# im2col, 3x3: one instruction for the copies of two channels, and one first load in place of two

## The chip, the cores and the metric

The kernel runs on one core of a Trainium2 chip. The metric is the device time of one execution in microseconds (us). The core has a vector engine (VectorE, DVE in the profile), a scalar engine (ScalarE, ACT), GpSimd (POOL), a sync engine (SyncE, SP) that here only issues transfers, and a matrix engine that this kernel doesn't use. Sixteen DMA engines move data between device memory (HBM) and the on-chip memory of 128 partitions. A transfer that SyncE or ScalarE issues is spread over all sixteen, eight partitions to each, and it is recorded in packets. Each of the sixteen has its own completion write, and whoever waits for a transfer waits for all sixteen.

## The reference

The input `x` has 16 images of 64 channels, 32 by 32, in float32. The output has, for every image and channel, nine planes of 30 by 30: plane `ki*3 + kj` is the channel's image shifted by `ki` rows and `kj` columns. Nothing is computed; every input element is copied up to nine times.

```
h_out = h - kernel_size + 1          # 30
w_out = w - kernel_size + 1          # 30
for b in range(batch):
    col_idx = 0
    for i in range(h_out):
        for j in range(w_out):
            patch = x[b, :, i:i + kernel_size, j:j + kernel_size].copy()
            cols[b, :, col_idx] = patch.ravel()
            col_idx += 1
```

The input is 4.19 MB and the output 33.18 MB.

## The kernel before

The 16 x 64 = 1024 channels are laid over the 128 partitions, eight consecutive channels to a partition (`CPP` = 8). A partition's input is one run of 32,768 bytes in HBM, and its output one run of 259,200 bytes. The whole input fits into one tile, `in_tile` (partition, channel, row, column). The output is built in four rounds, each for a pair of channels, in `out_tile` (partition, 2 channels, 9 planes, 30, 30): 64,800 bytes in a partition. There are two such buffers (line 26), so round 2 can't write until the store of round 0 is through, and round 3 waits for that of round 1.

The loads (lines 33 to 41). There are three: channel 0 of each partition, issued by SyncE; channel 1, issued by ScalarE; and channels 2 to 7, issued by SyncE. The first two are called `first` and are moved by hand, after the program is compiled, to the front of the program on their engines, ahead of the barrier with which all engines start (lines 88 to 103). The third is issued after that barrier.

The copies (lines 49 to 70). In a round, for each of the two channels `s`, ScalarE copies the three planes with `ki` = 1 in one instruction (line 55, 2700 elements in a partition). VectorE copies two planes of `ki` = 0 and two planes of `ki` = 2 (line 57, 1800 elements each). Planes 2 and 8, the third ones of `ki` = 0 and 2, are left. For the first channel VectorE takes both in one instruction (line 61); for the second, VectorE takes plane 2 (line 65) and ScalarE plane 8 (line 68). That makes six instructions on VectorE (9,900 elements) and three on ScalarE (6,300 elements), or nine in all for the 18 planes. The helper `planes` (lines 43 to 47) builds the source: `n` windows of 30 by 30 that lie `step` elements apart in one channel's image. The order is the one written, with no scheduler (line 28).

A wait is put on the first instruction that needs it: in round 0, the first channel's copies wait for the first load alone, and those of the second channel for the second load too. The copies of round 1 wait for the third load.

The store (line 71) is issued by SyncE once both engines have finished a round, one transfer of 8.29 MB. SyncE's queue thus holds, in this order: the load of channel 0, the load of channels 2 to 7, and four stores. ScalarE's holds the load of channel 1 only.

Of the kernel before, what the change touches and what calls it, by code (L numbers as in the profile page):

```python
# [1 line left out]

# [3 lines left out]


def _im2col(ctx, tc, x, K, out):


    nc = tc.nc
    P = nc.NUM_PARTITIONS

    B, C, H, W = x.shape
    HO = H - K + 1
    WO = W - K + 1
    KK = K * K
    assert out.shape == (B, C * KK, HO * WO)
    CPP = B * C // P
    assert CPP * P == B * C and C % CPP == 0 and CPP % 2 == 0 and K == 3  # L20

    x_v = x.rearrange("b (cp c2) h w -> (b cp) (c2 h w)", c2=CPP)
    out_v = out.rearrange("b (cp c2 kk) n -> (b cp) c2 (kk n)", c2=CPP, kk=KK)

    in_pool = ctx.enter_context(tc.tile_pool(name="in_pool", bufs=1))
    out_pool = ctx.enter_context(tc.tile_pool(name="out_pool", bufs=2))

    ctx.enter_context(tc.manual_schedule())

    in_tile = in_pool.tile([P, CPP, H, W], x.dtype, name="in_tile")  # L30
    in_flat = in_tile.rearrange("p c h w -> p (c h w)")

    def load(queue, r0, r1):

        return queue.dma_start(
            out=in_flat[:, r0 * W : r1 * W],
            in_=x_v[:, r0 * W : r1 * W],
        )

    first = load(nc.sync, 0, H), load(nc.scalar, H, 2 * H)  # L40
    load(nc.sync, 2 * H, CPP * H)

    def planes(c, ki, kj, n, step):

        w = in_tile[:, c, ki : ki + HO, kj : kj + WO]
        part, row, col = [list(d) for d in w.ap]
        return bass.AP(w.tensor, w.offset, [part, [step, n], row, col])

    for c in range(0, CPP, 2):
        out_tile = out_pool.tile([P, 2, KK, HO, WO], x.dtype, name="out_tile")  # L50


        for s in range(2):
            o = out_tile[:, s]
            nc.scalar.copy(out=o[:, K : 2 * K], in_=planes(c + s, 1, 0, K, 1))  # L55
            for ki in (0, 2):
                nc.vector.tensor_copy(  # L57
                    out=o[:, ki * K : ki * K + 2], in_=planes(c + s, ki, 0, 2, 1)
                )
            if s == 0:  # L60
                nc.vector.tensor_copy(  # L61
                    out=o[:, 2:KK:6], in_=planes(c + s, 0, 2, 2, 2 * W)
                )
            else:
                nc.vector.tensor_copy(  # L65
                    out=o[:, 2], in_=in_tile[:, c + s, 0:HO, 2 : 2 + WO]
                )
                nc.scalar.copy(  # L68
                    out=o[:, 8], in_=in_tile[:, c + s, 2 : 2 + HO, 2 : 2 + WO]
                )  # L70
        nc.sync.dma_start(  # L71
            out=out_v[:, c : c + 2].rearrange("p c n -> p (c n)"),
            in_=out_tile.rearrange("p c kk i j -> p (c kk i j)"),
        )
    return first


def kernel(
    tc: tile.TileContext,
    x: bass.AP,  # L80
    kernel_size: bass.AP,
    out: bass.AP,
):
    with ExitStack() as ctx:
        first = _im2col(ctx, tc, x, int(kernel_size), out)


    tc.close()
    tc.compile()  # L89
    blocks = tc.nc.main_func.blocks  # L90
    for load in (f.ins for f in first):
        home = next(
            b for b in blocks if any(i.name == load.name for i in b.instructions)
        )
        home.instructions = [i for i in home.instructions if i.name != load.name]
        head = list(blocks[0].instructions)
        at = next(
            k
            for k, i in enumerate(head)
            if i.engine == load.engine and type(i).__name__ == "InstDrain"  # L100
        )
        head.insert(at, load)
        blocks[0].instructions = head


# [1 line left out]
_INS = ['x', 'kernel_size']  # L107
_OUTS = [((16, 576, 900), 'float32')]

_NUMBERS = {'kernel_size': 3}  # L110


# [26 lines left out]
```

## Time and profile before

| | us |
|---|---|
| four runs | 91.31, 91.50, 91.51, 91.51 (median 91.50) |
| the profiled execution | 91.51 |
| its span, first to last instruction | 89.7 |
| VectorE busy / ScalarE busy | 22.6 (25%) / 23.8 (27%) |
| moved by the DMA engines | 37.37 MB, a mean of 417 GB/s over the span |

The span leaves out what lies around the first and the last instruction, 1.8 us here. In the rows of groups a line has the source line, the engine, the operation, the tiles, the shape (partitions x elements) and the count; behind the first bar the busy time of all in us and the mean duration of one in ns, behind the second the idle time just before them and what ended it. In the timeline a row has its start and its length in us, then the engine, the line and the operation; rows of one kind are merged, and a bracket says how long the engine had been idle and what ended that.

The DMA issues of the page, with the median time from issue to landing:

```profile
## 6 DMA issues: line engine op xcount, KB each, us to landing
out_dram<-out_tile SPq DMA_DIRECT2D x4, 8100.0 KB, 32.4
in_tile<-in_x_dram SPq DMA_DIRECT2D x1, 3072.0 KB, 11.4
in_tile<-in_x_dram SPq DMA_DIRECT2D x1, 512.0 KB, 4.4
in_tile<-in_x_dram ACTq DMA_DIRECT2D x1, 512.0 KB, 4.8
```

A store's time to landing holds the time that it waits in the queue behind the transfer before it.

### The profile page before, as it was taken

The numbers are of one execution on the slowest core, as the hardware profiler recorded it, in microseconds if no ns is written. First come the engines' busy times: TensorE is split into PE (matmuls) and PEld (weight loads), VectorE is DVE, ScalarE is ACT, GpSimd is POOL, SyncE is SP. The second block draws the span as 40 slices with busy tenths as digits, with TensorE's granted clock in tenths as the row PEclk, the third lists the DMA queues.
The fourth block names the chain that finished last, engine by engine and source line by source line (L and its number), as shares of the span: only waits on it lengthen the run. The fifth ranks groups of instructions, "written<-read, shape, count | busy, mean of one in ns | idle before, by whom it ended". The sixth has DMA issues, their size and how long they took to land.

```text
span 89.7 us, 97 instructions
## 1 busy us (share of the span) xinstructions
DVE 22.6 (25%) x24; ACT 23.8 (27%) x13; POOL 0.2 (0%) x4
## 2 busy tenths in 40 slices
DVE  0099459900000099600000399100000000000000
ACT  5099459900000099500000399100000000000000
POOL 0000000000000000000000000000000000000000
DMA  4989999999999999995699999999999999678990
GB/s 124 508 362 482 394 462 462 462 462 462 462 462 462 462 462 462 433 433 260 289 433 462 462 462 462 462 462 462 462 462 462 462 404 462 289 318 376 462 462 0
DMA packets 1008, 37.37 MB, mean 417 GB/s; under 512 B 112, under 2 KB 112, under 8 KB 368
## 3 DMA queue, kind: packets, MB, share of 16 engines
q1 hardware_dynamic: 864, 36.85, 95.5%
q10 hardware_dynamic: 144, 0.52, 1.4%
HBM read 4.19 MB, written 33.18 MB: 417 GB/s over the span
## 4 chain that ended last, share of the span: by engine, by line
DMA 49%; DVE 12%; DVEq 1%; issue 0%; SPq 0%
DMA out_dram<-out_tile 36%; DMA in_tile<-in_x_dram 13%; DVE out_tile L57 8%; DVE out_tile L61 2%; DVE out_tile L65 1%; DVEq L89 1%; DVEq L57 0%; SPq L71 0%
## 5 line engine op out<-in xcount | busy, mean ns | idle before, releaser
L55 ACT COPY out_tile<-in_tile 128x2700 f32<-128x2700 f32 x8 | 19.2, 2443 | 31.6 <-DMA out_dram<-out_tile 27.2
L57 DVE COPY out_tile<-in_tile 128x1800 f32<-128x1800 f32 x16 | 16.8, 1093 | 33.8 <-DMA out_dram<-out_tile 27.1
L61 DVE COPY out_tile<-in_tile 128x1800 f32<-128x1800 f32 x4 | 4.4, 1091 | 0.0
L68 ACT COPY out_tile<-in_tile 128x900 f32<-128x900 f32 x4 | 3.8, 938 | 0.0
L65 DVE COPY out_tile<-in_tile 128x900 f32<-128x900 f32 x4 | 2.5, 623 | 0.0
L55 ACT ACT_TABLE_LOAD x1 | 1.3, 1283 | 0.9 <-PEq L120 0.9
L120 POOL MEMSET const-bfloat16-1.0<- 128x1 bf16 x1 | 0.1, 102 | 0.0
L120 POOL MEMSET const-uint8-127<- 128x1 uint8 x1 | 0.1, 102 | 0.0
L120 POOL MEMSET const-float32-1.0<- 128x1 f32 x1 | 0.1, 99 | 0.0
L120 POOL MEMSET const-float32-0.0<- 128x1 f32 x1 | 0.1, 98 | 0.2 <-issue 0.2
## 6 DMA issues: line engine op xcount, KB each, us to landing
out_dram<-out_tile SPq DMA_DIRECT2D x4, 8100.0 KB, 32.4
in_tile<-in_x_dram SPq DMA_DIRECT2D x1, 3072.0 KB, 11.4
in_tile<-in_x_dram SPq DMA_DIRECT2D x1, 512.0 KB, 4.4
in_tile<-in_x_dram ACTq DMA_DIRECT2D x1, 512.0 KB, 4.8
```

The source lines that it names most:

```text
L55: nc.scalar.copy(out=o[:, K : 2 * K], in_=planes(c + s, 1, 0, K, 1))
L57: nc.vector.tensor_copy(out=o[:, ki * K : ki * K + 2], in_=planes(c + s, ki, 0, 2, 1))
L61: nc.vector.tensor_copy(out=o[:, 2:KK:6], in_=planes(c + s, 0, 2, 2, 2 * W))
L65: nc.vector.tensor_copy(out=o[:, 2], in_=in_tile[:, c + s, 0:HO, 2 : 2 + WO])
L68: nc.scalar.copy(out=o[:, 8], in_=in_tile[:, c + s, 2 : 2 + HO, 2 : 2 + WO])
L89: tc.compile()
L120: nc = _bacc.Bacc("TRN2", target_bir_lowering=False, num_devices=1)
```

## The change

The copies of a round become five instructions, four of which take one shape of window from more than one plane or channel:

- ScalarE: the three planes of `ki` = 1, both channels (5400 elements)
- VectorE: the three planes of `ki` = 0, both channels (5400 elements)
- VectorE: the first two planes of `ki` = 2, both channels (3600 elements)
- VectorE: the third plane of `ki` = 2, first channel (900 elements)
- ScalarE: the third plane of `ki` = 2, second channel (900 elements)

VectorE still copies 9,900 elements in a round and ScalarE 6,300. The helper `windows` takes the place of `planes`; its source has a loop over channels, one over windows, and rows and columns. The first load is one transfer of channels 0 and 1, issued by SyncE ahead of the barrier; ScalarE issues no transfer. The third load, the stores and the buffers are as they were. The first copies of round 0 on either engine read both channels, so they wait for the whole first load.

```
-    def load(queue, r0, r1):
+    def load(r0, r1):
-        return queue.dma_start(
+        return nc.sync.dma_start(
...
-    first = load(nc.sync, 0, H), load(nc.scalar, H, 2 * H)
-    load(nc.sync, 2 * H, CPP * H)
+    first = load(0, 2 * H)
+    load(2 * H, CPP * H)
-    def planes(c, ki, kj, n, step):
+    def windows(c, n, ki, kj, m):
-        w = in_tile[:, c, ki : ki + HO, kj : kj + WO]
-        part, row, col = [list(d) for d in w.ap]
-        return bass.AP(w.tensor, w.offset, [part, [step, n], row, col])
+        w = in_tile[:, c : c + n, ki : ki + HO, kj : kj + WO]
+        part, chan, row, col = [list(d) for d in w.ap]
+        return bass.AP(w.tensor, w.offset, [part, chan, [1, m], row, col])
...
-        for s in range(2):
-            o = out_tile[:, s]
-            nc.scalar.copy(out=o[:, K : 2 * K], in_=planes(c + s, 1, 0, K, 1))
...
+        for on_act, s, n, ki, kj, m in (
+            (True, 0, 2, 1, 0, K),
+            (False, 0, 2, 0, 0, K),
+            (False, 0, 2, 2, 0, 2),
+            (False, 0, 1, 2, 2, 1),
+            (True, 1, 1, 2, 2, 1),
+        ):
+            src = windows(c + s, n, ki, kj, m)
+            dst = out_tile[:, s : s + n, ki * K + kj : ki * K + kj + m]
+            if on_act:
+                nc.scalar.copy(out=dst, in_=src)
             else:
-                nc.vector.tensor_copy(
-                    out=o[:, 2], in_=in_tile[:, c + s, 0:HO, 2 : 2 + WO]
-                )
-                nc.scalar.copy(
-                    out=o[:, 8], in_=in_tile[:, c + s, 2 : 2 + HO, 2 : 2 + WO]
-                )
+                nc.vector.tensor_copy(out=dst, in_=src)
...
-    for load in (f.ins for f in first):
+    load = first.ins
```

The rest of the diff moves that one load to the front of the program in the way that two were moved.

More of the change, by code (lines that the diff above doesn't have):

```diff
@@ L38, in load @@
         )
-    first = load(nc.sync, 0, H), load(nc.scalar, H, 2 * H)
-    load(nc.sync, 2 * H, CPP * H)
-    def planes(c, ki, kj, n, step):
-        w = in_tile[:, c, ki : ki + HO, kj : kj + WO]
-        part, row, col = [list(d) for d in w.ap]
-        return bass.AP(w.tensor, w.offset, [part, [step, n], row, col])
+    first = load(0, 2 * H)
[4 more added lines that the diff above has]
+        return bass.AP(w.tensor, w.offset, [part, chan, [1, m], row, col])
     for c in range(0, CPP, 2):
         out_tile = out_pool.tile([P, 2, KK, HO, WO], x.dtype, name="out_tile")
-        for s in range(2):
-            o = out_tile[:, s]
[L55 to L58, printed above, removed]
-                )
-            if s == 0:
-                nc.vector.tensor_copy(
-                    out=o[:, 2:KK:6], in_=planes(c + s, 0, 2, 2, 2 * W)
-                )
-            else:
-                nc.vector.tensor_copy(
-                    out=o[:, 2], in_=in_tile[:, c + s, 0:HO, 2 : 2 + WO]
-                )
-                nc.scalar.copy(
-                    out=o[:, 8], in_=in_tile[:, c + s, 2 : 2 + HO, 2 : 2 + WO]
-                )
+        for on_act, s, n, ki, kj, m in (
[9 more added lines that the diff above has]
+                nc.scalar.copy(out=dst, in_=src)
+            else:
+                nc.vector.tensor_copy(out=dst, in_=src)
         nc.sync.dma_start(
@@ L90 @@
     blocks = tc.nc.main_func.blocks
-    for load in (f.ins for f in first):
[L92 to L103, printed above, removed]
+    load = first.ins
+    home = next(b for b in blocks if any(i.name == load.name for i in b.instructions))
+    home.instructions = [i for i in home.instructions if i.name != load.name]
+    head = list(blocks[0].instructions)
+    at = next(
+        k
+        for k, i in enumerate(head)
+        if i.engine == load.engine and type(i).__name__ == "InstDrain"
+    )
+    head.insert(at, load)
+    blocks[0].instructions = head
 _INS = ['x', 'kernel_size']
```

## The prediction

> **What bounds the kernel now.** I read the page's slices first, then the timeline, the DMA issues, and last the trace's records of single packets, because the page leaves one question open that only they answer. The slices of the page:
>
> ```profile
> DVE  0099459900000099600000399100000000000000
> ACT  5099459900000099500000399100000000000000
> DMA  4989999999999999995699999999999999678990
> ```
>
> The two copying engines are busy in four short bursts, one for each pair of channels, and the DMA row stays at 9 from the third slice to the end. The dips (56 and 678) are an effect of booking: a row of a store is one packet of 64,800 bytes that lasts 2.39 us, longer than a slice of 2.24 us. The packet records have all 512 of them between 2.391 and 2.427 us. So the transfers have no slack to be found in the middle. The timeline tells what waits for what:
>
> ```profile
> 0.00 1.24 SPq L35 DMA_DIRECT2D in_tile<-in_x_dram  x2
> 0.11 0.36 ACTq L35 DMA_DIRECT2D in_tile<-in_x_dram  x1
> 4.39 4.79 ACT L55 COPY out_tile<-in_tile 128x2700 f32<-128x2700 f32 x2 [2.21 <-DMA in_tile<-in_x_dram]
> 4.39 2.10 DVE L57 COPY out_tile<-in_tile 128x1800 f32<-128x1800 f32 x2 [4.39 <-DMA in_tile<-in_x_dram]
> 9.08 0.94 ACT L68 COPY out_tile<-in_tile 128x900 f32<-128x900 f32 x1
> 9.43 0.62 DVE L65 COPY out_tile<-in_tile 128x900 f32<-128x900 f32 x1
> 10.14 46.67 SPq L71 DMA_DIRECT2D out_dram<-out_tile  x4
> 12.29 2.10 DVE L57 COPY out_tile<-in_tile 128x1800 f32<-128x1800 f32 x2 [2.24 <-DMA in_tile<-in_x_dram]
> 31.58 4.79 ACT L55 COPY out_tile<-in_tile 128x2700 f32<-128x2700 f32 x2 [13.66 <-DMA out_dram<-out_tile]
> 50.72 4.79 ACT L55 COPY out_tile<-in_tile 128x2700 f32<-128x2700 f32 x2 [13.51 <-DMA out_dram<-out_tile]
> ```
>
> The reader is to see the only place where copies could hold up a transfer. Pair 0 is copied from 4.39 to 10.05 and its store is issued at 10.14, while the 3 MB load of the other channels still runs. By the packet records, that load's last packets end on the sixteen engines between 11.37 and 11.90, and the store's first packet follows on each engine 6 ns after the load's completion write: no gap on any. Pairs 1, 2 and 3 finish their copies at 17.95, about 37.3 and 56.4, and their stores' turn comes at about 31.0, 50.1 and 69.2 (the last landings, at 31.48, 50.62 and 69.76, less 0.5 us from last packet to landing). Some 13 us cover them. The last stores land 19.14 us apart. So the end is fixed by one number: when the slowest DMA engine starts its first store packet (11.90), plus four times 19.14, plus a tail. The last landing is at 88.91, the span 89.7, the profiled execution 91.51; the median of the runs shown is 91.50, so a sum on the one serves for the other.
>
> **The copies.** The durations are these rows:
>
> ```profile
> L55 ACT COPY out_tile<-in_tile 128x2700 f32<-128x2700 f32 x8 | 19.2, 2443 | 31.6 <-DMA out_dram<-out_tile 27.2
> L57 DVE COPY out_tile<-in_tile 128x1800 f32<-128x1800 f32 x16 | 16.8, 1093 | 33.8 <-DMA out_dram<-out_tile 27.1
> L61 DVE COPY out_tile<-in_tile 128x1800 f32<-128x1800 f32 x4 | 4.4, 1091 | 0.0
> L68 ACT COPY out_tile<-in_tile 128x900 f32<-128x900 f32 x4 | 3.8, 938 | 0.0
> L65 DVE COPY out_tile<-in_tile 128x900 f32<-128x900 f32 x4 | 2.5, 623 | 0.0
> ```
>
> VectorE: (1092 - 623)/900 = 0.521 ns an element and 0.154 us fixed; the next copy starts 0.086 us before the records' end of the one before (starts 1.006 us apart). Five copies of 1800 and one of 900 become one of 5400 (2.967, next after 2.881), one of 3600 (2.030, next after 1.944) and one of 900 (0.623): 5.45 us for a pair, against 10.05 - 4.39 = 5.66 now. ScalarE: (2443 - 938)/1800 = 0.836 ns and 0.186 us fixed, overlap 0.095. Two of 2700 and one of 900 become one of 5400 (4.700, next after 4.605) and one of 900 (0.938): 5.54 against 5.64. The elements are the same; only boundaries go. ScalarE now ends a pair, 0.12 us sooner. For pairs 1 to 3 this is worth nothing (cover of 13 us). For pair 0 it counts against a later start.
>
> No row has the two-channel pattern, with four loops in the source. The nearest is L61, whose two planes lie two image rows apart and which costs what L57 does, so I take the same rate. The bounds are a gain of the fixed parts alone, and a loss at ScalarE's rate or slower, which the rivals price.
>
> **The load.** The SyncE load of channel 0 landed on its last engine at 4.365 and both engines started 0.02 later. The ScalarE load of channel 1 landed at 4.962, and nobody waited: ScalarE reached channel 1 at 6.74. In the changed kernel each engine's first copy reads both channels and waits for all. Everything of pair 0 is queued behind it, and the first store behind that.
>
> When does the joint load land? Each DMA engine now moves 16 packets of 4,096 bytes at a step of 155 ns (2.48 us); packets of 24,576 bytes go at 908.5. On the line between, one of 8,192 costs 306, and eight 2.45, so 0.03 us less; one completion write of 6 ns goes too. Landing: 4.962 - 0.04 = 4.92. The engine-by-engine records also show a start-up loss: from the first packets at 1.01 to 1.35 until the 3 MB load's first at 4.07 to 4.63, each engine takes some 3.1 to 3.3 us for 2.48 us of packets, most of it in one or two slow early packets (up to 0.846 us where 0.159 is usual). I leave the loss as it is, as each engine seems to pay it once; half or all of it could go (0.3 to 0.6 us), or packets of twice the size could double it. The issue on ScalarE that goes took 0.365 us, beside POOL's memsets and the start barrier, ahead of a table load that ends 2.2 us before ScalarE's first copy: nothing. On SyncE's queue the 3 MB load stays behind one issue, at 0.90 or a little earlier, well before the first load is through.
>
> **What reaches the end.** Copies start at 4.94 and end at 4.94 + 5.54 = 10.48; the store is issued 0.09 later, at 10.57, 0.43 later than now. From issue to first packet the trace shows one uncovered case, the first load: issued at 0.00, packets from 1.01 to about 1.35 by engine. The store is then ready at 11.58 to 11.92. The load ahead of it ends on the engines at 11.34 to 11.86. The early engines wait about 0.25 us, which costs nothing, as they end half a microsecond ahead of the slowest one (landings of the last store from 88.38 to 88.91). The slowest engine waits up to 0.06. Sum: -0.04 + 0.06 = +0.02, or 91.53 us. Note that an earlier or later landing moves the load's end and the store's issue together, so it passes through whole, and the gap depends only on that latency: it opens above 1.29 us on the slowest engine.
>
> The latency's bounds: with 0 there is no gap, 91.47. The first store of the trace came without a gap, 1.24 us after its issue on the first engine and 1.76 on the last, so at most 1.76 there: a gap of 0.47, 91.94. I take 1.01 to 1.35, the only uncovered row.
>
> [...]
>
> **The rivals.** (1) *The first store finds the engines idle.* Price: the latency is nearer 1.76 than 1.35, or an engine that has gone idle pays a slow first packet once more (0.846 - 0.159 = 0.69 us). It decides once the slowest engine waits. For it: the store loses 0.43 us of a lead that was 1.24 to 1.76, and the slow packets stood at the start, after idleness. Against: the slowest engine loses its cover last. Time: from 91.7, where it can first be told from no change (a gap of 0.23), to a gap of 0.06 + 0.69 = 0.75, so 91.51 - 0.04 + 0.75 = 92.2. (2) *The start-up loss shrinks* since one queue brings larger packets: half of 0.6, passed through whole, 91.53 - 0.3 = 91.2 (to 91.0 if more goes). For it: slow packets come early, where now there will be half as many. Against: each engine shows it about once, whatever its count. (3) *VectorE loses half its rate* on the four-loop pattern: 9,000 elements at 1.042 ns are 4.7 us more, pair 0 ends near 15.1 instead of 10.48, and the end moves by about 4.6 us: 96.1. For it: nothing but that the form is new. Against: L61. [...] (4) *The edits don't take effect*: the built kernel has three VectorE and two ScalarE copies a pair and a single load ahead of the barrier, so this falls away.
>
> **How the numbers follow.** About 0.2% (0.18 us) is what a measurement tells from no change. The sum with its latency of 1.35 or less, 91.35 to 91.7: 0.44. Rival 1: 0.32. Rival 2: 0.20. Rival 3: 0.04. So faster 0.20, the same 0.44, slower 0.36. The predicted time is the likeliest case's 91.53. The range, 91.15 to 92.1, leaves out rival 3 and the far ends of rivals 1 and 2, less than 2 in 10 together; the likeliest case's own is 91.35 to 91.7.
>
> **What would show it.** Right: first copies near 4.94 on both engines, copies of 5400 at about 2.97 and 4.70 us, the first store issued near 10.57, its packets on early engines later than the load's end there, the slowest engine's near 11.9, and stores still 19.14 us apart. Rival 1 shows as a first store packet after 12.0 on the slowest engine, or one longer than 2.43 us. Rival 2 shows as a first copy before 4.75. A VectorE copy of 5400 above 4 us is rival 3. The prediction is wrong if the store's issue or the spacing of the stores moves for a cause not named here, such as the launch outside the span (91.51 - 89.7 = 1.8 us) changing with a queue left unused.

## The result, and the profile after

The changed kernel takes 91.31 us (median of 46 runs, 91.12 to 91.49), the kernel before 91.48 (median of 70 runs on the same chips). The ratio is 0.998, with a 95% interval of 0.9974 to 0.9986: 0.17 us faster, a little more than nothing, where 0.02 us slower was forecast.

The slices of the changed kernel's page, in the same rows as before:

```profile
span 89.5 us, 80 instructions
...
DVE  0089559800000099400000499000000000000000
ACT  5089659800000099500000499000000000000000
DMA  5989899999999999997499999999999999299990
```

The picture is the one of before: four bursts of copies under a DMA row that stands at 8 and 9 from the second slice to the last but one, dips aside. The dips (74 and 2) are again the booking of 2.39 us packets over slices of 2.24 us. The timeline of the changed kernel (start and length in us, engine, line, operation, and in brackets what ended the idle time before):

```profile
0.00 1.11 SPq L35 DMA_DIRECT2D in_tile<-in_x_dram  x2
...
0.77 1.28 ACT L63 ACT_TABLE_LOAD   x1 [0.77 <-PEq L113]
4.82 5.55 ACT L63 COPY out_tile<-in_tile 128x5400 f32<-128x5400 f32 x2 [2.76 <-DMA in_tile<-in_x_dram]
4.82 5.46 DVE L65 COPY out_tile<-in_tile 128x5400 f32<-128x5400 f32 x3 [4.82 <-DMA in_tile<-in_x_dram]
10.39 46.05 SPq L66 DMA_DIRECT2D out_dram<-out_tile  x4
12.09 5.46 DVE L65 COPY out_tile<-in_tile 128x5400 f32<-128x5400 f32 x3 [1.82 <-DMA in_tile<-in_x_dram]
...
31.39 5.54 ACT L63 COPY out_tile<-in_tile 128x5400 f32<-128x5400 f32 x2 [13.75 <-DMA out_dram<-out_tile]
...
50.53 5.54 ACT L63 COPY out_tile<-in_tile 128x5400 f32<-128x5400 f32 x2 [13.61 <-DMA out_dram<-out_tile]
```

Read it from the bottom. Rounds 2 and 3 start when stores 0 and 1 have landed, at 31.39 and 50.53, 0.19 us earlier than before (31.58 and 50.72). Round 1 starts at 12.09, 0.20 us earlier. So the gain is already there when the 3 MB load lands, and the rest is only carried along. Pair 0 starts 0.43 us later than before (4.82 against 4.39) and its store is issued 0.25 us later (10.39 against 10.14). The packet records say that this delay reaches nothing: the 3 MB load ends on the sixteen engines at 11.22 to 11.73, and the store's packets follow at once, but for two early engines that wait 0.03 to 0.04 us. On the slowest engine the first store packet starts at 11.73, where it was 11.90.

The groups of the changed kernel, shapes apart (busy us, mean ns):

```profile
L63 ACT COPY out_tile<-in_tile 128x5400 f32<-128x5400 f32 x4 | 18.8, 4702 | 31.8 <-DMA out_dram<-out_tile 27.4 <-DMA in_tile<-in_x_dram 4.5
L65 DVE COPY out_tile<-in_tile 128x5400 f32<-128x5400 f32 x4 | 11.9, 2974 | 34.2 <-DMA out_dram<-out_tile 27.6 <-DMA in_tile<-in_x_dram 6.6
L65 DVE COPY out_tile<-in_tile 128x3600 f32<-128x3600 f32 x4 | 8.1, 2029 | 0.0
```

The two-channel copies keep the rate of the one-channel copies: 2.97, 2.03 and 4.70 us, as worked out from the rows of before.

### The profile page after: what moved, and what is told of

Read it like the earlier page. It is cut to its first block, busy times and chain, and to the rows that moved or that the text cites. A ratio compares the mean times of both kernels' runs of the same rounds, so it can differ in the third digit from the quotient of the medians.

```text
span 89.5 us, 80 instructions
## 1 busy us (share of the span) xinstructions
DVE 21.8 (24%) x12; ACT 23.5 (26%) x9; POOL 0.2 (0%) x4
## 4 chain that ended last, share of the span: by engine, by line
DMA 49%; ACT 11%; ACTq 1%; issue 0%
DMA out_dram<-out_tile 37%; DMA in_tile<-in_x_dram 13%; ACT out_tile L63 11%; ACTq L84 1%; ACTq L63 0%
## 5 line engine op out<-in xcount | busy, mean ns | idle before, releaser
L63 ACT COPY out_tile<-in_tile 128x5400 f32<-128x5400 f32 (+1 forms) x8 | 22.2, 2821 | 31.8 <-DMA out_dram<-out_tile 27.4
L65 DVE COPY out_tile<-in_tile 128x5400 f32<-128x5400 f32 (+2 forms) x12 | 21.8, 1875 | 34.2 <-DMA out_dram<-out_tile 27.6
```

Of the source, the lines that this page charges most:

```text
L63: nc.scalar.copy(out=dst, in_=src)
L65: nc.vector.tensor_copy(out=dst, in_=src)
```

## The experiments

What was open: which half of the change brings the 0.17 us, and by what. The table has the packet records of one profiled execution each (the other columns) and the median time of each kernel. "Next load" is the first packet of the 3 MB load (or what takes its place) on the sixteen engines; "idle" is how long an engine had no packet under way between 1.5 and 2.1 us, a mean over sixteen; "extra" is what the first load's packets took beyond their usual length, a mean per engine; "start-up" is the mean of the next load less the first load's packets at their steady pace (per engine 16 at 155 ns, or 8 at 306, 456 and 607 for the larger sizes, which lie on the line between 155 and the 908.5 of the 3 MB load); "store" is the slowest engine's first store packet.

| kernel | first load, packets | idle | extra | next load, mean / slowest | start-up | store | time | time less store |
|---|---|---|---|---|---|---|---|---|
| before | two, 4,096 | 0.05 | 0.47 | 4.27 / 4.63 | 1.79 | 11.90 | 91.48 | 79.58 |
| after | joint, 8,192 | 0.00 | 0.48 | 4.16 / 4.46 | 1.71 | 11.73 | 91.31 | 79.58 |
| e1 | joint, 8,192 | 0.00 | 0.53 | 4.13 / 4.45 | 1.68 | 11.72 | 91.28 | 79.56 |
| e2 | two, 4,096 | 0.05 | 0.48 | 4.23 / 4.59 | 1.75 | 12.31 | 91.86 | 79.55 |
| e5 | two, 4,096 | 0.05 | 0.43 | 4.24 / 4.48 | 1.76 | 11.75 | 91.42 | 79.67 |
| e7 | joint, 4,096 | 0.10 | 0.42 | 4.33 / 4.50 | 1.85 | 11.77 | 91.46 | 79.69 |
| e10 | joint, 12,288 | 0.03 | 0.58 | 5.51 / 5.82 | 1.86 | 12.76 | 92.39 | 79.63 |
| e11 | joint, 16,384 | 0.04 | 0.64 | 6.77 / 7.03 | 1.91 | 14.00 | 93.58 | 79.58 |

The last column first: over times that differ by 2.3 us it stays within 79.55 to 79.69. It sets a median beside the records of one execution; with the profiled execution's own time in its place it is 79.52 to 79.69 in all twelve kernels of this document. The time is the slowest engine's first store packet plus 79.6, as the prediction's sum had it. Everything else is about what moves that packet.

**e1: the joint load with the nine old copies.** The edit, against the kernel before:

```
-    first = load(nc.sync, 0, H), load(nc.scalar, H, 2 * H)
+    first = (load(nc.sync, 0, 2 * H),)
```

> The nine copies of the kernel before, with the joint first load of the changed kernel. Theory A (the whole gain is in the first load: the start-up of the DMA engines costs less, the 3 MB load ends earlier, and everything behind it moves along): the first landing near 4.80, first store packets on the slowest engine near 11.73, time 91.3, ratio to the kernel before 0.998. Pair 0 ends near 4.82 + 5.66 = 10.48, the store is issued near 10.57 and is ready after 0.86 more, at 11.43, still ahead of the slowest engine's 11.73. Rival B (the merged copies matter, since they let the first store be issued earlier): without them the gain is gone, 91.45 to 91.6, ratio 0.9995 or more.

Measured: 91.28 us beside 91.45, ratio 0.9977 (0.9967 to 0.9986). Its timeline:

```profile
4.81 4.79 ACT L55 COPY out_tile<-in_tile 128x2700 f32<-128x2700 f32 x2 [2.75 <-DMA in_tile<-in_x_dram]
4.81 2.10 DVE L57 COPY out_tile<-in_tile 128x1800 f32<-128x1800 f32 x2 [4.81 <-DMA in_tile<-in_x_dram]
...
9.85 0.62 DVE L65 COPY out_tile<-in_tile 128x900 f32<-128x900 f32 x1
10.56 7.62 SPq L71 DMA_DIRECT2D out_dram<-out_tile  x2
```

The store is issued at 10.56, 0.17 us later than with merged copies, and starts on the early engines at 11.42 instead of 11.25. They wait, and the slowest engine does not: 11.72. The whole gain is in the load, and merging the copies brings nothing to the time. Rival B falls.

**e2 and e5: the merged copies with the two loads.** The edit of e2, against the changed kernel (the lines that move the first loads are those of the kernel before), and what e5 adds ahead of the copies:

```
-    first = load(0, 2 * H)
+    first = load(nc.sync, 0, H), load(nc.scalar, H, 2 * H)
...
+    warm = in_pool.tile([P, 2], x.dtype, name="warm")
+    nc.vector.memset(warm[:, 0:1], 0.0)
+    nc.scalar.copy(out=warm[:, 1:2], in_=warm[:, 0:1])
```

> The five merged copies, with the two first loads of the kernel before on two queues. Theory A (the gain is in the first load): as the kernel before, 91.48, ratio 1.000; copies start near 4.98, the store is issued near 10.55 and starts with no gap on the slowest engine, near 11.9. Rival B (the merged copies bring it): 91.3, ratio 0.998.

> The merged copies and two first loads on two queues once more, but with a copy of one element on ScalarE ahead of them (VectorE zeroes its source), so that the activation table is loaded near 0.9 and not after the wait for the first load. Theory A (the gain is in the first load; the 0.4 us that the run without this lost is the late table load alone, which held the first store until the engines stood idle): the store is issued near 10.65, is ready 0.85 later at 11.5, and the slowest engine takes it without a gap at 11.86 to 11.90: as the kernel before, 91.45, ratio 1.000. Rival (merged copies cannot be had with two loads: the store is late anyway, or the idle engines cost it): 91.7 or more.

Measured: e2 91.86, ratio 1.0039 (1.0025 to 1.0054), a loss that neither theory had. The timeline of e2:

```profile
4.45 1.28 ACT L63 ACT_TABLE_LOAD   x1 [4.45 <-DMA in_tile<-in_x_dram]
5.02 5.45 DVE L65 COPY out_tile<-in_tile 128x5400 f32<-128x5400 f32 x3 [5.02 <-DMA in_tile<-in_x_dram]
5.74 5.54 ACT L63 COPY out_tile<-in_tile 128x5400 f32<-128x5400 f32 x2
11.31 6.93 SPq L66 DMA_DIRECT2D out_dram<-out_tile  x2
```

The first copies now wait for two loads, and on ScalarE one of the two waits stands ahead of the table load: it starts at 4.45, where it had started near 0.9, and its 1.28 us come on top. ScalarE begins at 5.74 instead of 5.02, and the store is issued at 11.31. The DMA engines have all finished the 3 MB load by 11.86 and stand idle until the store's packets start at 12.16 to 12.31. In e5 a one-element copy brings the table load forward:

```profile
0.90 1.28 ACT L45 ACT_TABLE_LOAD   x1 [0.90 <-PEq L119]
...
4.89 5.54 ACT L67 COPY out_tile<-in_tile 128x5400 f32<-128x5400 f32 x2 [2.50 <-DMA in_tile<-in_x_dram]
...
10.46 7.66 SPq L70 DMA_DIRECT2D out_dram<-out_tile  x2
```

e5: 91.42 beside 91.47, ratio 0.9995 (0.9981 to 1.0009), the same as before. So the two loads with either set of copies give the time of before, and the joint load with either set gives 0.998. By the way, e2 shows what a late store costs: 0.44 us over e5 by the medians. In the two profiled executions the slowest first packet is 0.56 us later, and the time 0.57 longer (91.92 against 91.35).

**e3 and e6: two loads of one channel on one queue.** The edits are `first = load(nc.sync, 0, H), load(nc.sync, H, 2 * H)` on e2 and on e5.

> The five merged copies, with two first loads of one channel each, both on SyncE's queue: packets of 4,096 bytes as before, one queue as after. If the gain comes from the packets being twice as large (half as many packets meet the slow start): as the kernel before, 91.45, ratio 0.9995, the 3 MB load's first packets up to 4.63. If it comes from there being one queue only (no second transfer set up 1.1 us later, no turns between two queues): as the changed kernel, 91.3, ratio 0.998, the 3 MB load's first packets up to 4.45.

> The same early table load, with both first loads on SyncE's queue (packets of 4,096 bytes, one queue). If the single queue brings the gain: 91.3, ratio 0.998. If the packet size brings it: 91.45, ratio 1.000. A third: the 3 MB load, which is issued 0.48 us later behind two issues ahead of the barrier, again has slow packets (up to 1.7 us) after its start and ends near 12.8 on the slowest engine: 92.3 to 92.5, ratio 1.010.

Measured: 92.42 (ratio 1.0105, 1.0088 to 1.0122) and 92.32 (1.0098, 1.007 to 1.0125). In e3 the table load is late again (5.16), and the 3 MB load's end and the store's start meet near 12.87. In e6 the table is loaded early and the store is issued at 10.69, so the third case of its expectation is what is left: 20 packets of the 3 MB load are slow, up to 1.51 us where 0.91 is usual, most of them between 5 and 6.5 us, and it ends at 11.80 to 12.82. That load was issued at 1.27 instead of 0.90 or 0.78. Why its packets then run slow stays open, and these two runs don't decide between packet size and queue.

**e4: halves of the partitions on two queues.** Two queues with packets of 8,192 bytes, which was to separate the two differences.

```
-    first = load(0, 2 * H)
+    def half(queue, p0, p1):
+        return queue.dma_start(
+            out=in_flat[p0:p1, 0 : 2 * H * W], in_=x_v[p0:p1, 0 : 2 * H * W]
+        )
+    first = half(nc.sync, 0, P // 2), half(nc.scalar, P // 2, P)
...
```

> The five merged copies, with the first load as two halves of 64 partitions, both channels in each row, one half on SyncE's and one on ScalarE's queue: packets of 8,192 bytes as after, two queues as before. If the gain comes from the larger packets: 91.3, ratio 0.998. If it comes from the single queue: 91.45 to 91.5, ratio 0.9995 or more.

Measured: 93.79, ratio 1.0251 (1.0235 to 1.0266), and no answer. The packets of the halves took a median of 539 and 607 ns where 309 is usual for that size, the second half landed at 7.38, and the first store's packets start at 13.81 to 14.12. The packets of the first half start at 1.32 to 3.53 us and those of the second at 3.09 to 5.89, so the halves came largely one after the other, and by the medians a packet took nearly twice its usual time. Why is not shown.

**e7: the joint load in small packets.** 32 bytes are left free between channels 0 and 1 in the input tile, so the row of 8,192 bytes becomes two of 4,096.

```
...
+    two = in_tile[:, 0:HW]
+    two = bass.AP(
+        two.tensor, two.offset, [list(two.ap[0]), [HW + PAD, 2], [1, HW]]
+    )
...
+    first = nc.sync.dma_start(
+        out=two, in_=x_v[:, 0 : 2 * HW].rearrange("p (c n) -> p c n", c=2)
+    )
...
```

> The changed kernel with 32 bytes left free between channel 0 and channel 1 of the input tile, so that the joint first load, one transfer on one queue, goes in packets of 4,096 bytes. If the larger packets bring the gain: 91.45, ratio 0.9995 to 1.000, the 3 MB load's first packets up to 4.6. If it is the single transfer on a single queue: 91.3, ratio 0.998, up to 4.47.

Measured: 91.46 beside 91.47, ratio 0.9997 (0.9985 to 1.0008). Its timeline:

```profile
0.00 0.43 SPq L39 DMA_DIRECT2D in_tile<-in_x_dram  x1
...
4.89 5.54 ACT L71 COPY out_tile<-in_tile 128x5400 f32<-128x5400 f32 x2 [2.78 <-DMA in_tile<-in_x_dram]
...
10.46 7.64 SPq L74 DMA_DIRECT2D out_dram<-out_tile  x2
```

One transfer on one queue, but in packets of 4,096 bytes, has lost the gain, though its interval and that of the changed kernel (0.9974 to 0.9986) just touch. So a single transfer on a single queue does not bring the gain by itself. The edit doesn't separate the size of the packets from what came with it: the issue took 0.43 us (0.37 in the changed kernel), the first packet started at 1.09 (1.00), and in the table e7 has the most idle time.

**e9: rows side by side.** The guess was that the slow early packets come from rows 32 KB apart.

```
-    x_v = x.rearrange("b (cp c2) h w -> (b cp) (c2 h w)", c2=CPP)
-    out_v = out.rearrange("b (cp c2 kk) n -> (b cp) c2 (kk n)", c2=CPP, kk=KK)
+    x_v = x.rearrange("b c h w -> (b c) (h w)").rearrange(
+        "(r p s) n -> p r (s n)", p=P, s=2
+    )
+    out_v = out.rearrange("b (c kk) n -> (b c) (kk n)", kk=KK).rearrange(
+        "(r p s) n -> p r (s n)", p=P, s=2
+    )
...
```

The indices of the loads and the stores follow from that.

> The changed kernel with other channels in a partition: round r has the pairs r*128 to r*128+127, one to a partition, so that the first load reads 1 MB in one run of HBM (a row every 8 KB instead of every 32 KB) and each store writes 8.29 MB in one run. The third load goes in 8,192-byte packets, 24 on an engine, 0.08 us more by the rates of this case. If the slow first packets (0.46 to 0.98 us where 0.31 is usual) come from rows 32 KB apart meeting in one part of HBM: they vanish, the 3 MB load starts 0.3 to 0.5 us sooner, 90.9 to 91.1. If they are the engines' own start: they stay, 91.35 to 91.4.

Measured: 91.48, ratio 0.9994 (0.9983 to 1.0006). Each of the sixteen engines still has one slow packet, and it is longer (0.77 us extra against 0.48). The guess falls. The time is 0.1 us above what was expected of the engines' own start. It also shows that one transfer in packets of 8,192 bytes is not enough for the gain: here the engines had no idle time between 1.5 and 2.1 us either, but with the longer slow packets they came to the next load at a mean of 4.32 us (4.16 in the changed kernel).

**e10 and e11: three and four channels in the first load.** The edits are `load(0, 3 * H)` and `load(0, 4 * H)`, with the next load starting there.

> The changed kernel with three channels in the first load (packets of 12,288 bytes) and five in the next. Two questions. (a) Start-up: the mean of the sixteen engines' first packets of the next load, less eight packets at 456 ns (3.65 us), was 1.79 us with packets of 4,096 bytes (4.27 - 2.48, kernel before) and 1.71 with 8,192 (4.16 - 2.45, changed kernel). If engines lack packets in the first microsecond and larger ones fill that, it falls further, to 1.62 to 1.70; if a slow packet costs in proportion to its size, it rises above 1.75. (b) The price of a late first store: pair 0 ends near 11.5, the store is issued near 11.6 and its packets start 0.85 to 1.0 later, 12.45 to 12.6, when all engines have been idle for 0.7 to 1.2 us. If the wait is all that it costs, the time is 12.6 + 79.6 (from the slowest engine's first store packet to the end, as in the changed kernel: 91.31 - 11.73) = 92.2. If idle engines pay a slow first packet again, as rival 1 of the prediction priced it: 92.7 to 92.9.

> The same with four channels in the first load (packets of 16,384 bytes, 607 ns, eight of them 4.86 us). (a) The start-up part is 1.60 to 1.70 us, so the next load's first packets have a mean of 6.46 to 6.56; in proportion to size it would be above 1.8. (b) Pair 0 ends near 12.75, the store's packets start at 13.7 to 13.85, and the time is 93.4 if the wait is all, 93.9 or more with a slow first packet.

Measured: 92.39 (ratio 1.0098, 1.0077 to 1.0119) and 93.58 (1.0229, 1.0209 to 1.025). On (a) both missed: the start-up part rises to 1.86 and 1.91. The engines' idle time is small, but the slow packet grows with its size, from 0.47 us extra to 0.58 and 0.64. So 8,192 bytes is the best of the four sizes tried (a start-up of 1.71 against 1.79, 1.86 and 1.91), and "larger is better" is wrong; beyond 8,192 bytes the first load itself is larger too, and these runs don't tell size from amount. On (b) the wait is all that a late store costs. The timeline of e11:

```profile
7.44 10.99 ACT L63 COPY out_tile<-in_tile 128x5400 f32<-128x5400 f32 x4 [5.36 <-DMA in_tile<-in_x_dram]
7.44 10.82 DVE L65 COPY out_tile<-in_tile 128x5400 f32<-128x5400 f32 x6 [7.44 <-DMA in_tile<-in_x_dram]
13.00 5.79 SPq L66 DMA_DIRECT2D out_dram<-out_tile  x2
```

The engines have finished their loads by 11.89, the store is issued at 13.00, and its packets start at 13.85 to 14.00 and take 2.42 to 2.44 us, 0.04 more than usual: no slow start. The slowest first packet plus 79.6 gives 92.36 and 93.60, against 92.39 and 93.58 measured.

## Why the prediction was wrong

Its forecast was no change, at 91.53 with a range of its own of 91.35 to 91.7. The time lies just below that, and inside the wide range only because that left room for rival 2. Two terms of the sum failed: the start-up loss, left as it is, shrank and gave -0.17 in place of -0.04, and the latency of the first store, taken as up to 1.35 us, was 1.00 at most where a run uncovered it, and added nothing in place of +0.06. By its own signs the first copies came at 4.82, neither near 4.94 nor before rival 2's 4.75. Point by point:

- *What bounds the kernel: right.* Slowest engine's first store packet plus a constant. In all twelve kernels that constant is 79.52 to 79.69 by the profiled executions, and the first packet's position decides.
- *The copies: right.* 5.46 and 5.54 us a pair (5.45 and 5.54 worked out), at no loss of rate, which rules out rival 3, and worth nothing to the time (e1, e5).
- *The joint landing: the term that was mis-sized.* "I leave the loss as it is" gave -0.04; the profile has 4.962 - 4.797 = -0.165 for the last landing, and the 3 MB load's first packet came 0.17 us earlier on the slowest engine and 0.11 on the mean. With the like runs beside them the means are 4.23 to 4.27 for two loads (before, e2, e5) and 4.13 to 4.16 for the joint one (after, e1).
- *What the joint load gained.* For before against after, the mean's 0.11 is made up as far as the records go: 0.03 from the packets' pace and 0.006 from a completion write, as predicted; 0.05 from engines that between 1.5 and 2.1 us had no packet under way in the kernel before and were never idle there in the changed one; the slow packets count 0.01 the other way, and the last 0.04 is within what such records differ by. The other 0.06 of the slowest engine's 0.17 is not accounted for; in single executions with two loads its first packet came at 4.48 to 4.63. The reason that I gave, that each engine pays the loss once, holds for the slow packets and overlooks the idle time. That the gain goes with the joint load is shown (e1, e5), and e7 speaks for its needing the long rows as well; why the engines lack packets in the first microsecond stays open (in e3 and e6, also with 4,096 bytes, they were idle for 0.01 and 0.03).
- *The latency of the first store: too long.* I took 1.01 to 1.35 us from the only uncovered case, a load. Where a store's start was uncovered (e2, e3, e10, e11) it was 0.85 us on the first engine and 0.99 to 1.00 on the last. So the gap of 0.06 on the slowest engine does not open, and the sum is -0.17 and not +0.02.
- *Rival 1: its mechanism exists, its price was wrong, and it did not decide.* In e2 the store did find all engines idle, from 11.86 to 12.16 us. The price is the wait alone (e10, e11); the slow packet of 0.69 us that I added was not paid by the store (2.42 to 2.44 us a packet in e11, against 2.39).
- *Rival 2: the right outcome, from half a reason.* It said 91.2, and 91.0 if more went. But there are not half as many slow packets: counted as those over 0.1 us longer than usual, 19 before and 18 after, with 0.47 and 0.48 us extra an engine. What went, as far as the records show it, is idle time between packets.

## What to carry to other kernels

When a kernel is one unbroken stream of transfers, look for the one packet that fixes the end and ask of every edit only what it does to that packet; here first copies that start 0.43 us later are free, and a next load that starts 0.17 us earlier on the slowest engine brings 0.17 us. The first load's packet size is worth a try in both directions: from 8,192 bytes and a start-up of 1.71 us, halving it (e7, the same amount, 1.85) and doubling it (e11, twice the amount, 1.91) both cost more at the start. And when an instruction gets a second thing to wait for, look where its engine's set-up work then stands: in e2 the table load went behind the first wait, from 0.90 to 4.45 us.

## What the runs showed of the hardware that was not expected

- A ScalarE copy with two loads to wait for had its table load put behind the first wait: 4.45 us instead of 0.90, and 0.44 us in the time (e2 against e5).
- The first load had about one slow early packet per engine at each of the four sizes tried, 4,096 to 16,384 bytes (outside e4, 16 to 26 of them on sixteen engines, 0.42 to 0.77 us extra an engine). The first store's packets that started after a wait of 0.3 to over 2 us had none (2.41 to 2.44 us each against 2.39; e2, e10, e11).
- Two halves of 64 partitions on two queues moved 8,192-byte packets in 539 and 607 ns, against 309 for 128 partitions in one transfer (e4); why is not shown.
- With two loads issued by SyncE ahead of the barrier, some of the third load's packets were slow, most of them between 4 and 6.3 us, and its slowest engine ended 0.9 to 1.0 us later than before (e3, e6); the cause was not looked for.
